# A hybrid transformer on one core: 64 unused bytes on the left of SBUF and 96 on the right shift every tile

## The chip, the cores and the metric

One core of a Trainium2 chip runs the whole program in one launch. The metric is the device time of that core in microseconds (us), as a median of several executions; lower is better. A profile of one execution gives start and duration of every instruction on TensorE (PE for its matmuls, PEld for its weight loads), VectorE (DVE), ScalarE (ACT) and GpSimd (POOL), and the transfers of the DMA queues.

## The reference

Two layers of a transformer on 512 tokens with 1024 features, all in float32. Each layer is a half-weighted feed-forward network (FFN), a mixer, and a second half-weighted FFN, each behind an RMS norm. The first mixer joins gated linear attention (4 heads) with forgetting attention (8 heads); the second is sparse attention in a latent space (16 heads, a top-k of the keys).

```python
def swiglu(h, w_in, w_out):
    a, b = jnp.split(h @ w_in, 2, axis=-1)
    return (jax.nn.silu(a) * b) @ w_out          # w_in 1024 x 5632, w_out 2816 x 1024
...
    for layer in range(DEPTH):
        g = norm_g[layer]
        x = x + 0.5 * swiglu(rmsnorm(x, g[0]), ffn_w_in[layer, 0], ffn_w_out[layer, 0])
        h = rmsnorm(x, g[1])
        x = x + (even_mixer if layer % 2 == 0 else odd_mixer)(h, ...)
        x = x + 0.5 * swiglu(rmsnorm(x, g[2]), ffn_w_in[layer, 1], ffn_w_out[layer, 1])
    return rmsnorm(x, final_norm_g)
```

(The loop is shortened: the two mixers take weights of their own.)

## The kernel before, in words

The stages run one after the other: FFN 0, even mixer, FFN 1, FFN 2, odd mixer, FFN 3, final norm. Tokens lie along the free dimension of a tile, features on the 128 partitions.

**Three products for one.** An operand is split into a high part of type float32r (a rounded float32 that TensorE takes at its full rate) and a low part, and a product is the sum of high x high, high x low and low x high. `mm3` (line 204) issues these three for the FFN's down product and for the mixers' projections; the FFN's up product does the same at line 366. Weights are fetched by SP's queue into raw tiles (`wraw`, `a`), split by ScalarE (`whi`) and VectorE (`wlo`, lines 84 and 88, 162 and 163), and become the stationary operand. Each matmul is preceded by a weight load of its own.

**The FFN's up product** is a seven-product scheme for 2x2 blocks: eleven rounds (pairs of hidden tiles), each with seven products `p1` to `p7` of 24 matmuls over 256 columns, all of them from line 366. Their moving operands are the tiles `th` and `tl` (high and low part of the input blocks). **The down product** multiplies the tiles `hh` and `hl` in matmuls over 512 columns (lines 207 to 209).

**The mixers** first project: the input `xgh`, `xgl` is the moving operand over 512 columns, or, for values, the stationary one with the weights moving over 256 columns. Attention and output products follow; their tiles are called `x`, `p` and `pts`.

**Where tiles lie.** A partition of SBUF is filled from both ends. Pools on the left are stacked upwards: the pool `one` (residual `X`, gains `gn` of 224 bytes, `ones`, `ident`, masks, `cols` of 32 bytes), then the small tiles of the norms, then `wraw`, `wsp` (which holds `whi` and `wlo`), and in their stage `hp` (`hh`, `hl`) or the mixers' pools. The one pool on the right, `xp`, hangs from the upper end: `th` and `tl`, or `xgh` and `xgl`, the raw weight tiles `a` and the work tiles `ws`, `te`, `to`. Small tiles are no multiples of 128 bytes, so that what follows them starts between two multiples. In the program before, `X` starts at byte 16,512, `ss` at 35,200, and the highest tile of the right side ends at byte 229,344 of its partition.

Where an operand starts, modulo 128 bytes, for all 12,006 matmuls of the program:

| matmuls (type, columns that move) | count | stationary, moving before |
|---|---|---|
| FFN up, float32r, 256 | 7,224 | 64, 96 |
| FFN down, mixers' `x` tiles, float32r, 512 | 2,640 | 64, 64 |
| projections of `xgh`/`xgl` (720) and FFN 0's first products (96), float32r, 512 | 816 | 64, 96 |
| mixers' values, float32r, 256 (stationary `xgh`/`xgl`) | 384 | 96, 64 |
| other float32r (scores, narrow projections) | 240 | 64, 64 or 96, 96, narrow ones mixed |
| float32 (transposes, attention values, norms) | 702 | mixed |

Of the kernel before, what the change touches and what calls it, by code (L numbers as in the profile page):

```python
# [8 lines left out]
F32 = mybir.dt.float32  # L9
# [163 lines left out]
class Builder:  # L173
# [1090 lines left out]
    def build(self):  # L1264
        from contextlib import ExitStack
        with ExitStack() as ctx:
            nc, tc = self.nc, self.tc
            pool = lambda name, bufs, **kw: ctx.enter_context(tc.tile_pool(name=name, bufs=bufs, **kw))
# [6 lines left out]
            self.pp = pool("pp", 1, space=PSUM)  # L1275
            self.dram = pool("dram", 1, space=bass.MemoryType.DRAM)
            one = lambda name, shape, dt=F32: self.one.tile(shape, dt, name=name)
            self.lnexp()
            self.X = one("X", [128, KT, S])
            self.gn = one("gn", [128, 7, KT])  # L1280
# [7 lines left out]
            for t, n in ((self.chunkmask, "chunkmask"), (self.ident, "ident"), (self.causal, "causal"), (self.cols, "cols")):  # L1288
                nc.gpsimd.dma_start(t, self.i[n])

            self.xp = None

            def open_in(kind):
# [173 lines left out]
```

## Time and profile before

| | before |
|---|---|
| median of three runs | 1914.0 us (1907.32 to 1915.86) |
| profiled execution, its own time | 1906.54 us |
| its span in the profile | 1904.7 us |
| instructions in the profile | 30516 |
| mean granted TensorE clock | 0.991 |

The span is what the profiler sees from the first to the last instruction; the execution's own time has some 2 us around it. A granted clock of 1 is the upper of TensorE's two levels (2.4 GHz), 0.5 the lower (1.2 GHz). The duration that the profile gives for one matmul contains its way through the array and overlaps with the next one's: what a matmul costs in a dense stretch is the distance from its start to the start of the next.

### The profile page before, as it was taken

Reading aid. Unit: us, or ns where it says so; the run is one execution under the profiler, and the core shown is the slowest. Engines: PE = TensorE matmul, PEld = TensorE weight load, DVE = VectorE, ACT = ScalarE, POOL = GpSimd, SP = SyncE. Lnnn points to the kernel's source line nnn. Section 1 sums busy time; section 2 is a strip of 40 time slices with the busy share of each in tenths; the row PEclk is TensorE's granted clock in tenths of the full one; section 3 lists DMA queues with packets and bytes.
Section 4 is the critical chain, followed back from the end, with each engine's and each line's share of the span. In section 5 each row is a group of like instructions: output and inputs, shape, how many; then the busy total and the mean of one; then the engine's idle time right before and its main releaser. Section 6 shows DMA issues by size and latency. Waiting matters only on the chain.

```text
span 1904.7 us, 30516 instructions
## 1 busy us (share of the span) xinstructions
PE 1858.3 (98%) x12376; PEld 1665.6 (87%) x12376; DVE 1451.5 (76%) x1917; ACT 909.9 (48%) x1286; POOL 218.0 (11%) x211
## 2 busy tenths in 40 slices
PE   8999999999999999999999999999999999999997
PEld 7989899887877999989899998987777789899996
DVE  8979687457557979868897885964898599696774
ACT  6535345334465634525564452543538566353353
POOL 0000000100262000000200000011258320000001
PEclk9999999999999999999999999999999999999998
DMA  5333422223441233322423333234156222423322
GB/s 186 96 107 105 126 86 78 94 80 96 126 122 67 89 110 104 113 97 78 144 89 92 109 100 122 67 107 136 60 162 170 79 94 93 125 89 114 108 67 78
DMA packets 60653, 198.16 MB, mean 104 GB/s; under 512 B 7896, under 2 KB 8072, under 8 KB 57440
## 3 DMA queue, kind: packets, MB, share of 16 engines
q1 hardware_dynamic: 57856, 191.65, 32.2%
q10 hardware_dynamic: 2304, 4.20, 0.8%
q8 instruction: 97, 1.59, 0.3%
q0 software_dynamic: 352, 0.36, 0.1%
q14 instruction: 44, 0.36, 0.1%
HBM read 178.03 MB, written 2.15 MB: 95 GB/s over the span
## 4 chain that ended last, share of the span: by engine, by line
PE 84%; DVE 12%; ACT 2%; issue 1%; DMA 1%; SPq 0%; DVEq 0%; POOL 0%; ACTq 0%; POOLq 0%
PE ps L366 25%; PE pt L366 12%; PE s L209 6%; PE s L208 6%; PE s L207 6%; PE s L366 6%; PE ps L207 3%; PE ps L208 3%; PE ps L209 3%; PE s L730 2%; DVE tl L241 2%; DVE wlo L88 1%; PE o L764 1%; DVE acc L1217 1%; PE pt L749 1%; PE pt L207 1%
## 5 line engine op out<-in xcount | busy, mean ns | idle before, releaser
L366 PE MATMUL ps<-th,wlo 128*128 128x256 f32 x1376 | 384.8, 280 | 2.4 <-DVE wlo L163 2.3
L366 PE MATMUL ps<-th,whi 128*128 128x256 f32 x1376 | 385.2, 280 | 1.3 <-DVE ta L414 1.3
L366 PE MATMUL ps<-tl,whi 128*128 128x256 f32 x1376 | 384.5, 279 | 0.9 <-DVE tl L241 0.9
L84 ACT ACTIVATE whi<-wraw 128x1024 fp32r<-128x1024 f32 (+3 forms) x156 | 157.3, 1010 | 351.0 <-PE s L208 135.5
L366 PEld LDWEIGHTS ps<-th,wlo 128*128 128x128 f32 x1376 | 259.4, 188 | 3.2 <-DVE wlo L163 3.2
L366 PEld LDWEIGHTS ps<-th,whi 128*128 128x128 f32 x1376 | 259.2, 188 | 2.3 <-DVE ta L414 1.5
L366 PEld LDWEIGHTS ps<-tl,whi 128*128 128x128 f32 x1376 | 259.3, 188 | 1.7 <-DVE tl L241 1.1
L209 PE MATMUL s<-hh,wlo 128*128 128x512 f32 x528 | 205.9, 390 | 0.0
L208 PE MATMUL s<-hl,whi 128*128 128x512 f32 x528 | 205.6, 389 | 0.0
L207 PE MATMUL s<-hh,whi 128*128 128x512 f32 x528 | 205.6, 389 | 0.0
L162 ACT ACTIVATE whi<-a 128x1024 fp32r<-128x1024 f32 x131 | 139.0, 1061 | 137.8 <-issue 39.2
L88 DVE TENSOR_TENSOR wlo<-wraw,whi 128x1024 fp32r<-128x1024 f32 (+3 forms) x144 | 169.2, 1176 | 40.3 <-ACT whi L84 39.8
L279 POOL TENSOR_TENSOR ss<-ss,sq 128x512 f32<-128x512 f32 x41 | 65.4, 1596 | 1113.6 <-ACT sq L275 1113.4
L366 PE MATMUL pt<-th,whi 128*128 128x256 f32 x688 | 192.0, 279 | 0.0
L366 PE MATMUL pt<-tl,whi 128*128 128x256 f32 x688 | 191.9, 279 | 0.0
L366 PE MATMUL pt<-th,wlo 128*128 128x256 f32 x688 | 191.9, 279 | 0.0
L163 DVE TENSOR_TENSOR wlo<-a,whi 128x1024 fp32r<-128x1024 f32 x131 | 159.7, 1219 | 6.8 <-ACT whi L162 6.7
L162 ACT ACTIVATE whi<-wraw 128x1024 fp32r<-128x1024 f32 (+1 forms) x89 | 93.6, 1052 | 131.7 <-PE ps L366 51.5
L492 DVE SCALAR_TENSOR_TENSOR dn<-s,R 128x512 f32<-128x512 f32 x72 | 49.7, 690 | 122.3 <-PE s L209 122.3
L162 ACT ACTIVATE whi<-ws 128x1024 fp32r<-128x1024 f32 x86 | 90.7, 1055 | 84.0 <-PE ps L366 51.2
L366 PEld LDWEIGHTS pt<-tl,whi 128*128 128x128 f32 x688 | 129.3, 188 | 0.0
L366 PEld LDWEIGHTS pt<-th,wlo 128*128 128x128 f32 x688 | 129.3, 188 | 0.0
(323 smaller groups left out, 4338.4 us busy)
## 6 DMA issues: line engine op xcount, KB each, us to landing
a<-in_ffn_in_dram SPq DMA_DIRECT2D x88, 512.0 KB, 3.7
wraw<-in_ffn_in_dram SPq DMA_DIRECT2D x87, 512.0 KB, 4.7
wraw<-in_ffn_out_dram SPq DMA_DIRECT2D x64, 512.0 KB, 3.6
wraw<-in_ffn_out_dram SPq DMA_DIRECT2D x32, 384.0 KB, 3.1
x<-x SPq DMA_DIRECT2D x62, 128.0 KB, 2.3
wraw<-in_even_fox_dram SPq DMA_DIRECT2D x4, 1024.0 KB, 4.8
wraw<-in_even_out_dram SPq DMA_DIRECT2D x4, 1024.0 KB, 5.6
wraw<-in_odd_q_dram SPq DMA_DIRECT2D x8, 512.0 KB, 3.2
```

Of the source, the lines that this page charges most:

```text
L84: nc.scalar.activation(hi, x, AF.Copy)
L88: nc.vector.tensor_sub(lo, x, hi.bitcast(F32))
L162: b.nc.scalar.activation(o[0][:, s], x[:, s], AF.Copy)
L163: b.nc.vector.tensor_sub(o[1][:, s], x[:, s], o[0][:, s].bitcast(F32))
L207: mm(ps, w[0], x[0], start=first, stop=False)
L208: mm(ps, w[0], x[1], start=False, stop=False)
L209: mm(ps, w[1], x[0], start=False, stop=last)
L241: v.tensor_sub(l, src, h.bitcast(F32))
L279: nc.gpsimd.tensor_tensor(self.ss, self.ss, sq, op=OP.add)
L366: mm(o, w[:, c], x, start=fresh and f == j == i == 0, stop=j == 3 and i == 2, skip_group_check=True)
L492: nc.vector.scalar_tensor_tensor(t, bank, 0.5, R, op0=OP.mult, op1=OP.mult)
L730: nc.tensor.matmul(s[:, :n], q[hh][:, b * 128:b * 128 + 128], k[hh][:, :n], start=k is kh, stop=k is kl)
```

## The change

Two tiles are added that no instruction writes or reads. `edge_l` is the first tile of the pool `one`, 16 float32 = 64 bytes of each partition, and pushes all tiles of the left side up by 64 bytes. `edge` lies in a pool of its own on the right side, 24 float32 = 96 bytes, opened ahead of `xp`, and pushes all tiles of the right side down by 96 bytes.

```diff
             one = lambda name, shape, dt=F32: self.one.tile(shape, dt, name=name)
+            one("edge_l", [128, 16])
             self.lnexp()
             self.X = one("X", [128, KT, S])
...
+
+            pool("edge", 1, side="right").tile([128, 24], F32, name="edge")
             self.xp = None
```

Each engine has the same instructions in the same order with the same waits as before; only addresses in SBUF differ (PSUM and DRAM are as before). `X` now starts at byte 16,576, the highest tile on the right ends at 229,248, a multiple of 128. Of the table above, the first four rows and nearly all of the fifth now have stationary and moving operand at 0, 0: all 11,064 matmuls of the first four rows and 210 of the fifth's 240; the other 30 (of the projections 48 and 72 columns wide) start their stationary operand at another multiple of 32 bytes, their moving operand at 0 too. Operands of float32 moved as well, and not all of them to a multiple: `ident` goes from 96 to 32, `ones` from 96 to 32, `ss` from 0 to 64. `X`, which ScalarE, VectorE and GpSimd use and TensorE doesn't, goes from 0 to 64.

## Rows read from the trace of the kernel before

**Rows 1.** The page: engines' busy time, and the chain that ended last, by engine.
```profile
PE 1858.3 (98%) x12376; PEld 1665.6 (87%) x12376; DVE 1451.5 (76%) x1917; ACT 909.9 (48%) x1286; POOL 218.0 (11%) x211
...
PE 84%; DVE 12%; ACT 2%; issue 1%; DMA 1%; SPq 0%; DVEq 0%; POOL 0%; ACTq 0%; POOLq 0%
```

**Rows 2.** Stretches of time: length, busy us by engine, granted clock, DMA share, GB/s.
```profile
350.00:610.00 260.00, 253.98 (x1513) 207.07 (x1512) 156.28 (x273) 118.26 (x223) 57.02 (x80) 0.99 0.31 98
...
841.00:900.00 59.00, 59.00 (x479) 57.79 (x478) 50.59 (x51) 30.08 (x33) 0.00 (x0) 1.00 0.20 64
...
1300.00:1560.00 260.00, 245.26 (x1406) 194.12 (x1405) 204.01 (x455) 140.30 (x309) 112.47 (x93) 0.97 0.42 118
```

**Rows 3.** Groups by line and shape: count, busy us, mean ns, idle before.
```profile
L366 PE MATMUL ps<-th,whi 128*128 128x256 f32 x1376 | 385.2, 280 | 1.3 <-DVE ta L414 1.3
...
L209 PE MATMUL s<-hh,wlo 128*128 128x512 f32 x528 | 205.9, 390 | 0.0
...
L207 PE MATMUL ps<-xgh,whi 128*128 128x512 f32 x208 | 84.2, 405 | 0.0
...
L207 PE MATMUL ps<-whi,xgh 128*128 128x256 f32 x128 | 37.6, 294 | 0.0
```

**Rows 4.** Timeline of PE, FFN up, first and last of 34 matmuls.
```profile
1800.09 0.28 PE L366 MATMUL pt<-th,wlo 128*128 128x256 f32 x1
...
1803.94 0.28 PE L366 MATMUL ps<-th,wlo 128*128 128x256 f32 x1
```

**Rows 5.** Timeline of PE, even mixer's output product, first and last of 28 matmuls.
```profile
599.76 0.39 PE L207 MATMUL ps<-x,whi 128*128 128x512 f32 x1
...
605.88 0.39 PE L207 MATMUL ps<-x,whi 128*128 128x512 f32 x1
```

**Rows 6.** Timeline of PE, even mixer's projections, first and last of 58 matmuls.
```profile
439.65 0.40 PE L207 MATMUL ps<-xgh,whi 128*128 128x512 f32 x1
...
452.95 0.39 PE L207 MATMUL ps<-xgh,whi 128*128 128x512 f32 x1
```

**Rows 7.** Timeline of PE, even mixer's values, first and last of 38 matmuls.
```profile
381.28 0.28 PE L209 MATMUL ps<-whi,xgl 128*128 128x256 f32 x1
...
385.66 0.28 PE L207 MATMUL ps<-whi,xgh 128*128 128x256 f32 x1
```

**Rows 8.** Stretches: 512 columns at the lower clock; FFN up with transfers under way.
```profile
1359.90:1360.80 0.90, 0.90 (x3) 0.66 (x2) 0.58 (x1) 0.06 (x1) 0.00 (x0) 0.50 0.00 0
...
1800.00:1804.00 4.00, 4.00 (x37) 4.00 (x36) 3.30 (x4) 1.64 (x3) 0.00 (x0) 1.00 0.79 266
```

**Rows 9.** Timeline of PE at that lower clock, first and last of 3 matmuls.
```profile
1359.98 0.63 PE L207 MATMUL ps<-x,whi 128*128 128x512 f32 x1
...
1360.84 0.47 PE L209 MATMUL ps<-x,wlo 128*128 128x512 f32 x1
```

**Rows 10.** Timeline of PE, begin of FFN 0's down product: matmuls 1, 4 and 10.
```profile
93.51 0.40 PE L207 MATMUL s<-hh,whi 128*128 128x512 f32 x1
...
94.21 0.39 PE L207 MATMUL s<-hh,whi 128*128 128x512 f32 x1
...
95.57 0.39 PE L207 MATMUL s<-hh,whi 128*128 128x512 f32 x1
```

**Rows 11.** Timeline of PE, odd mixer: scores of 256 columns between projections.
```profile
1328.70 0.40 PE L1227 MATMUL s<-x 128*128 128x256 f32 x2
1328.94 0.40 PE L207 MATMUL ps<-xgh,whi 128*128 128x512 f32 x1
```

**Rows 12.** Timeline of PE, a norm's sums: one moving column each, eight weight loads.
```profile
624.06 0.95 PE L314 MATMUL o<-ones,ss 128*128 128x1 f32 x8
624.96 0.39 PE L366 MATMUL ps<-th,whi 128*128 128x256 f32 x1
```

## The prediction

> **What bounds the kernel now.** I read the page first. TensorE is busy for 98% of the span, VectorE for 76%, and 84% of the chain that ended last is matmuls [rows 1]. By stretches, an FFN's up product keeps TensorE busy without a gap at a granted clock of 1.00 (59.00 of 59 us), while VectorE has 50.59 us, 86%; the stretch with the even mixer leaves 260 - 254 = 6 us free, the one with the odd mixer 260 - 245 = 15 us [rows 2]. So the time is a count of matmuls times the distance between their starts, and the next engine is 14% away where most of them lie. Four groups of shapes hold 11,064 of the 12,006 matmuls [rows 3]; their operand offsets are in the table above.
>
> The timeline gives the distance of each group.
> - FFN up, 256 columns, offsets 64 (stationary) and 96 (moving): (1803.94 - 1800.09) / 33 = 116.7 ns [rows 4].
> - Output product, 512 columns, offsets 64 and 64: (605.88 - 599.76) / 27 = 226.7 ns [rows 5].
> - Projections, 512 columns, offsets 64 and 96: (452.95 - 439.65) / 57 = 233.3 ns [rows 6].
> - Values, 256 columns, offsets 96 and 64: (385.66 - 381.28) / 37 = 118.4 ns [rows 7].
>
> The second and third line are the finding. Same shape, same stationary offset, same clock; the moving operand at 96 instead of 64 costs 6.7 ns, 3%. At 2.4 GHz the three regular streams are 280, 544 and 560 cycles: per 32 columns (128 bytes) 35, 34 and 35. 560 is twice 280, so at offset 96 a column costs the same at either width, and the moving operand sets the pace there, not the weight load, which is 128 columns in both. At the lower clock the extra vanishes: 512 columns at a granted 0.50 take (1360.84 - 1359.98) / 2 = 430 ns, 516 cycles of 1.2 GHz within the rounding of the rows [rows 8, 9]. So in the dense streams something that feeds TensorE, not the array, is the limit, and the offset is part of it. Transfers are not: the 116.7 ns stand in a stretch with 266 GB/s under way [rows 4, 8].
>
> **The change part by part.** No instruction is added, removed or moved, no wait and no DMA; two idle tiles take memory alone and cost nothing. What changes is the offset of operands, group by group.
>
> FFN up, 7,224 matmuls: (64, 96) becomes (0, 0). No row shows an operand of float32r at 0. The nearest is a pair with equal offsets, 64 and 64, at 34 cycles per 32 columns; I take that rate, since a shift of both operands by the same 64 bytes leaves their distance as it is. 256 columns then take 226.7 / 2 = 113.3 ns, 3.3 ns less: 7,224 x 3.33 = 24.1 us. From below the gain is 0, if at 256 columns the next weight load sets the pace. From above the weight load by itself bounds it: with one moving column, eight loads take (624.96 - 624.06) / 8 = 112 ns each [rows 12], so at most 4.7 ns and 34 us.
>
> Projections, 816 matmuls: 233.3 becomes 226.7 ns by the rows that differ in nothing else. 96 of them open FFN 0, where TensorE waits for its operands; I count the other 720: 4.8 us.
>
> Values, 384 matmuls: 118.4 becomes 113.3 ns, as above: 1.9 us.
>
> Down and output products, 2,640 matmuls: (64, 64) becomes (0, 0). By the rate that I took: nothing. The bound below is a loss: such a stream needs some matmuls to reach its pace, (94.21 - 93.51) / 3 = 233.3 ns for the first three of a down product and (95.57 - 94.21) / 6 = 226.7 ns for the next six [rows 10]; if it never settled, 2,640 x 6.7 = 17.6 us would be lost. The bound above is an array that is never held up, 512 / 2.4 = 213.3 ns: 13.4 x 2,640 = 35 us won.
>
> [...]
>
> The rest: float32 operands, 702 matmuls, of which the transposes' `ident` goes from 96 to 32, lie in attention, where TensorE has its idle time; ScalarE's and VectorE's operands move too, but VectorE's 14% and ScalarE's half of the time cover a change of some per cent there. I count neither. If VectorE's cover were gone, that is its rate became 14% worse, a round of the FFN would wait for it.
>
> Sum: 24.1 + 4.8 + 1.9 = 30.8 us of TensorE. An FFN up round has 168 matmuls, 19.6 us; at 19.0 us VectorE's 86% become 88%, so no new bound arises, but waits at stage ends and in the two mixers don't shrink; I take 30. Against the profiled execution's own 1906.5 us (span 1904.7) that is 1876.5. That execution lies 7.5 us below the median of the runs, 1914.0, and half a per cent (some 9.6 us) is about what a measurement of this kernel can tell from no change, its three runs being 8.5 us apart. Against the median: **1884 us**.
>
> **The rivals.**
> - *Zero is better than 64.* If the surplus of 2 cycles per 32 columns comes from a boundary at each multiple of 128 bytes that a moving operand at 64 or 96 straddles, it falls or goes at 0. For: 34 and 35 of 32 show a surplus to be had, and it is larger for the worse offset. Against: no row has offset 0, and (64, 64) may already be the aligned case. With half of the surplus gone, 220 ns for 512 columns and the load's 112 ns for 256: 6.7 x 2,640 + 13.3 x 720 + 4.7 x 7,224 + 6.4 x 384 = 17.7 + 9.6 + 34.0 + 2.5 = 64 us, **1850 us**; with all gone 35 + 14.4 + 34 + 2.5 = 86 us, 1828. [...]
> - *The weight load paces the 256-column stream.* Then FFN up stays at 116.7 ns and only projections and values gain, 6.7 us: **1907 us**, within half a per cent. For: a pair of 256-column matmuls at 64 and 64 in the odd mixer takes (1328.94 - 1328.70) / 2 = 120 ns, no less than at 96 [rows 11], and the values, whose moving operand is at 64, take 118.4 [rows 7]. Against: the pair stands alone between projections, and streams need three matmuls to settle [rows 10]; the values' stationary operand is at 96; and 280 is exactly half of 560.
> - *Offsets have nothing to do with it*, and the 6.7 ns come from something else: **1914 us**. For: every tile at 64 lies on the left side, every one at 96 on the right, so side and offset are not told apart here. Against: tiles of different pools, stages and writers agree, `x` with `hh` at 226.7 ns [rows 5, 10], `xgh` with `th` at one cost per column [rows 4, 6].
> - *The 512-column streams no longer settle* at (0, 0), and the up product gains nothing: + 17.6 us, **1932 us**, slower. It decides from some 1,440 of the 2,640 matmuls on (9.6 us at 6.7 ns). For it: the pace depends on how two streams fall together, since it changes within nine matmuls [rows 10]. Against: the distance of the two offsets, the one thing that could set it, stays 0.
>
> **How the numbers follow.** The forecast has a chance of 0.42, zero better than 64 0.20, the load as the pace 0.22, no effect 0.05, never settled 0.11. Faster by over 0.5% are the first two, 0.62; within it the next two, 0.27; slower 0.11. The forecast's own range is 1875 to 1893 (31 us less a few, and the scatter of the runs). To leave out no more than 2 in 10, the range runs from 1840, which holds half or more of the second case, to 1912, which holds the third: below it some 0.07 are left, above it the last case and part of the fourth.
>
> **What would show it.** Right: in the profile after, 113.3 ns between starts of the up product's matmuls, 226.7 in projections, output and down products alike, VectorE's share in the up product near 88%, and the same instruction counts. 112 or less at 256 columns, and under 226 at 512, show the second case; 116.7 at 256 with 226.7 at 512 in the projections the third. Wrong would also be a distance that falls as said while the time doesn't, with new idle time ahead of line 366 released by VectorE.

## The result: 0.8% slower

| | before | after |
|---|---|---|
| median | 1912.96 us (4 runs, 1907.32 to 1915.86) | 1929.03 us (4 runs, 1925.98 to 1929.58) |
| profiled execution, its own time | 1906.54 us | 1929.58 us |
| its span | 1904.7 us | 1927.8 us |
| instructions | 30516 | 30516 |

The ratio is 1.0084, with an interval of 1.0058 to 1.011: slower by more than the half per cent that can be told from no change. The forecast was 1884 us, faster by 1.6%.

The page of the changed kernel, busy time by engine and the chain that ended last:

```profile
PE 1881.4 (98%) x12376; PEld 1689.4 (88%) x12376; DVE 1454.0 (75%) x1917; ACT 909.9 (47%) x1286; POOL 217.0 (11%) x211
...
PE 84%; DVE 11%; ACT 2%; issue 1%; DMA 1%; POOL 0%; SPq 0%; DVEq 0%; ACTq 0%; POOLq 0%
```

Against [rows 1] TensorE is busy 23.1 us longer with the same number of instructions, and the span is 23.1 us longer; VectorE, ScalarE and GpSimd stay within 3 us. The busy time of as many matmuls grew, and not the gaps between them: the same matmuls stand farther apart. Which of them, the timeline of TensorE shows (start, duration), the first and last of 34 matmuls of the up product, 28 of the output product, 58 of the projections and 38 of the values, as in [rows 4 to 7]:

```profile
1821.22 0.28 PE L366 MATMUL pt<-th,wlo 128*128 128x256 f32 x1
...
1825.18 0.28 PE L366 MATMUL ps<-th,wlo 128*128 128x256 f32 x1
...
606.69 0.39 PE L208 MATMUL ps<-x,whi 128*128 128x512 f32 x1
...
612.81 0.39 PE L208 MATMUL ps<-x,whi 128*128 128x512 f32 x1
...
440.57 0.39 PE L208 MATMUL ps<-xgl,whi 128*128 128x512 f32 x1
...
453.81 0.40 PE L208 MATMUL ps<-xgl,whi 128*128 128x512 f32 x1
...
383.75 0.28 PE L208 MATMUL ps<-wlo,xgh 128*128 128x256 f32 x1
...
388.14 0.28 PE L209 MATMUL ps<-whi,xgl 128*128 128x256 f32 x1
```

- FFN up: (1825.18 - 1821.22) / 33 = 120.0 ns, where [rows 4] gave 116.7.
- Output product: (612.81 - 606.69) / 27 = 226.7 ns, as in [rows 5].
- Projections: (453.81 - 440.57) / 57 = 232.3 ns, against 233.3 in [rows 6]; an unbroken run of 168 in the odd mixer has a mean of 233.3 ns in both kernels.
- Values: (388.14 - 383.75) / 37 = 118.6 ns, against 118.4 in [rows 7].

That the 120.0 ns hold throughout a stretch is seen by counting. In 60 us of FFN 1's up product, windows of the kernel before and of the changed one (columns as in [rows 2]):

```profile
740.00:800.00 60.00, 60.00 (x517) 60.00 (x516) 53.66 (x54) 33.82 (x38) 0.00 (x0) 1.00 0.33 102
```
```profile
740.00:800.00 60.00, 60.00 (x502) 60.00 (x501) 54.57 (x54) 32.68 (x36) 0.00 (x0) 1.00 0.30 97
```

A window of 60 us touches (60 + 0.28) / pace matmuls, so 517 is 116.6 ns and 502 is 120.1, both without a gap and at a granted clock of 1.00. This window is the measure used for the kernels below.

Where the 23 us arose, by stages, each from the start of its first product to the start of the next stage's, FFN 3 to the start of its last down product (from the timelines; one execution of each kernel, the experiments of the next section included):

```
            FFN 0   even    FFN 1+2   odd     FFN 3  | FFNs     mixers
before      347.1   261.3   679.7     256.8   338.5  | 1365.3   518.1
after       350.1   265.8   690.7     256.4   343.6  | 1384.4   522.2
l64         348.3   265.5   684.2     256.4   341.4  | 1373.9   521.9
r32         350.5   260.1   690.0     257.1   344.2  | 1384.7   517.2
r96         345.1   267.3   678.1     257.3   337.8  | 1361.0   524.6
same32      347.4   264.1   679.6     256.0   338.4  | 1365.4   520.1
r96m        346.0   264.5   678.4     259.8   337.7  | 1362.1   524.3
r96k        340.3   265.8   671.7     258.3   335.5  | 1347.5   524.1
d32k        345.8   267.5   678.9     259.5   338.7  | 1363.4   527.0
```

The FFNs took 19.1 us more, the mixers 4.1. An FFN has 1,176 up matmuls behind a down product, at 120.0 instead of 116.7 ns, and some 500 more behind its norm, at 118.8 instead of 116.8 (means that include a long first step): 3.9 + 1.0 = 4.9 us, and FFN 3 took 5.1 more. The windows behind FFN 1's norm, before and after:

```profile
645.00:690.00 45.00, 45.00 (x388) 45.00 (x387) 40.44 (x40) 24.20 (x27) 0.00 (x0) 1.00 0.32 100
```
```profile
645.00:690.00 45.00, 45.00 (x382) 45.00 (x381) 42.45 (x43) 27.18 (x30) 0.00 (x0) 1.00 0.25 82
```

The 4.5 us of the even mixer are within scatter: d32k, whose mixers lie at the addresses of before, took 267.5 us for it where before took 261.3. The profiled executions are 23 us apart and the medians 16, because the profiled one of before lies 6.4 us below its median and that of after 0.6 above.

### The profile page after: what moved, and what is told of

It reads as the page before. It is cut to its first block, busy times and chain, and to the rows that moved or that the text cites. A ratio compares the mean times of both kernels' runs of the same rounds, so it can differ in the third digit from the quotient of the medians.

```text
span 1927.8 us, 30516 instructions
## 1 busy us (share of the span) xinstructions
PE 1881.4 (98%) x12376; PEld 1689.4 (88%) x12376; DVE 1454.0 (75%) x1917; ACT 909.9 (47%) x1286; POOL 217.0 (11%) x211
## 4 chain that ended last, share of the span: by engine, by line
PE 84%; DVE 11%; ACT 2%; issue 1%; DMA 1%; POOL 0%; SPq 0%; DVEq 0%; ACTq 0%; POOLq 0%
PE ps L366 25%; PE pt L366 12%; PE s L207 6%; PE s L209 6%; PE s L208 6%; PE s L366 6%; PE ps L207 3%; PE ps L208 3%; PE ps L209 3%; PE s L730 2%; DVE tl L241 1%; PE o L764 1%; DVE wlo L88 1%; DVE acc L1217 1%; PE pt L749 1%; PE pt L207 1%
## 5 line engine op out<-in xcount | busy, mean ns | idle before, releaser
L366 PE MATMUL ps<-th,wlo 128*128 128x256 f32 x1376 | 391.1, 284 | 2.3 <-DVE wlo L163 2.3
L366 PE MATMUL ps<-tl,whi 128*128 128x256 f32 x1376 | 389.9, 283 | 0.0
L366 PEld LDWEIGHTS pt<-th,whi 128*128 128x128 f32 x688 | 130.4, 190 | 0.0
```

Of the source, the lines that this page charges most:

```text
L366: mm(o, w[:, c], x, start=fresh and f == j == i == 0, stop=j == 3 and i == 2, skip_group_check=True)
```

## The experiments

Three theories of what sets the pace of a dense stream. **Own offset**: where each operand starts modulo 128 bytes, as the prediction had it. **Side**: which end of SBUF it lies at. **Distance**: the start of the moving operand minus that of the stationary one, modulo some power of two. Of the third the change did something that its table of offsets modulo 128 doesn't show. It pushed the left side up by 64 and the right side down by 96, so the distance of the up product went from 32 to 32 - 160 = -128, which modulo 256 is 128; both operands start at multiples of 128 bytes now, but one at an even, the other at an odd multiple. The projections go from 32 to 128 with it; the values, whose stationary operand is the one on the right, go from 224 to 128. Output and down products have both operands on the left, and stay at 0.

**A map of the pace (map1).** Streams of 36 matmuls from line 53, with no work for another engine between them; 256 or 512 columns, distance 0 to 992 bytes in steps of 32, some with both operands shifted by the same `a`, some with the moving operand 82 KB away (the code is shortened, its constants written out).

```python
for name, n, d, a in streams():
    w0 = PADF + a // 4
    m0 = PADF + a // 4 + 2048 + d // 4
    for i in range(36):
        c = w0 + (i % 8) * 128
        nc.tensor.matmul(ps[:, :n], big[:, c:c + 128], big[:, m0:m0 + n], start=i == 0, stop=i == 35)
```

> A kernel of dense matmul streams alone (36 matmuls each, one weight load per matmul, no other engine at work); it computes nothing of the reference and writes its input out. Stationary chunks start at multiples of 512 bytes, the moving operand d bytes further modulo 1024, d from 0 to 992 in steps of 32, with 256 and with 512 columns; further streams shift both operands by 32, 64 and 96 bytes at d = 0, or put the moving operand 82 KB away. Theory 'distance': the pace is set by d alone, with some period; d = 0, 32 and 384 at 512 columns repeat the kernels' 226.7, 233.3 and 233.3 ns, d = 32 and 384 at 256 columns their 116.7 and 120.0 ns, and shifting both operands changes nothing. Theory 'own offset': the streams with both operands shifted by 32, 64, 96 differ from each other by 3 to 7 ns at 512 columns, and d matters only through the moving operand's own offset modulo 128, so the pace repeats every 128 bytes. Theory 'side': with both operands in one tile all streams run at 226.7 ns, and only the far ones at 233.3.

Measured: rows of the timeline, one for a whole stream (start, time from its first start to its last end). The name gives columns, distance and `a`:

```profile
30.51 4.43 PE L53 MATMUL n256d128a0x<-big 128*128 128x256 f32 x36
39.00 4.28 PE L53 MATMUL n256d192a0x<-big 128*128 128x256 f32 x36
421.07 4.47 PE L53 MATMUL n256d000a64x<-big 128*128 128x256 f32 x36
433.89 4.48 PE L53 MATMUL n256far000x<-big 128*128 128x256 f32 x36
149.27 8.35 PE L53 MATMUL n512d000a0x<-big 128*128 128x512 f32 x36
157.46 8.57 PE L53 MATMUL n512d032a0x<-big 128*128 128x512 f32 x36
```

Less the last one's duration (0.28 us, and 0.39 and 0.40 at 512 columns) and over 35 steps: 118.6 and 114.3 ns at 128 and 192, 119.7 with both operands at 64 modulo 128, 120.0 with the moving operand 82 KB away; (8.35 - 0.39) / 35 = 227.4 ns for 512 columns at distance 0, 233.4 at 32. Worked out from the last 16 steps of each stream, in ns:

```
distance modulo 256       0      32     64     96     128    160    192    224
256 columns             120.0  117.6  117.8  120.1  118.7  117.3  113.3  118.3
512 columns             226.7  233.3  228.9  233.6  233.3  234.7  233.3  233.3
```

The distances up to 992 repeat this row four times, all but the very first stream (distance 0, 256 columns), which took 7.23 us, a mean of 198.6 ns a step, and is left out; the first matmuls of the kernel before are slow too, (8.57 - 7.29) / 3 = 427 ns for 512 columns in a window with a granted clock of 1.00. Shifting both operands by 32, 64 or 96 at distance 0 changes nothing (120.0 and 226.7 ns), and being 82 KB apart changes less than half a nanosecond. So own offset and side fall, and distance modulo 256 bytes stands. Two things didn't come out as the theory of distance had it: 32 and 128 gave 117.6 and 118.7 ns at 256 columns where the kernels have 116.7 and 120.0, and with both operands shifted by 64 the stream at 32 ran at 116.7. So a distance can have more than one rate, which the experiments below take up. The map also contradicts what the prediction took for granted, that the two widths go together. Distance 0 is the best for 512 columns and among the two slowest for 256.

**One pad alone (l64, r96, r32).** The whole kernel with the left pad alone (distance of the up product 224), with the right pad alone (192), and with 32 bytes on the right instead of 96, which puts both operands at 64 modulo 128 and the distance at 0: in all stages, the pair of equal offsets that the prediction took for its rate. The three lines, one for each kernel in this order, against before:

```diff
+            one("edge_l", [128, 16])
...
+            pool("edge", 1, side="right").tile([128, 24], F32, name="edge")
...
+            pool("edge", 1, side="right").tile([128, 8], F32, name="edge") 
```

> The left pad alone: stationary at 0, moving at 96 in the up product (distance 480 modulo 512), 512-column down product at 0 and 0. Theory 'own offset, stationary at 0 is slow': up product at 120 ns, time as after the change, 1929 us. Theory 'own offset, moving at 0 is slow': 116.7 ns, 1913 us. Theory 'distance': the up product takes a value of its own that the map shows at d = 480; down product unchanged at 226.7.

> The right pad alone: stationary at 64, moving at 0 in the up product (distance 448 modulo 512), down product at 64 and 64. Theory 'own offset, stationary at 0 is slow': 116.7 ns, 1913 us. Theory 'own offset, moving at 0 is slow': 120 ns, 1929 us. Theory 'distance': the value of the map at d = 448.

> A right pad of 32 bytes alone: both operands of all large groups at 64 modulo 128, and their distance 0 modulo 512. Theory 'distance': up product and projections take the pace of the output products, 226.7 ns at 512 columns and so 113.3 at 256, 30 us won, 1883 us; if the weight load paces the 256-column stream, up to 120 ns there and 24 us lost, less 5 won in the projections, 1932 us. Theory 'own offset': since 64 and 64 is as bad or good as the mean of the two single shifts, between 1913 and 1929 us. Theory 'side': no change, 1913 us.

Measured: l64 1919.57 us, ratio 1.0056 (1.0038 to 1.0073); r96 1908.45 us, 1.0003 (0.9989 to 1.0017); r32 1928.62 us, 1.0108 (1.0079 to 1.0136). The window of the up product in l64, then r32:

```profile
740.00:800.00 60.00, 60.00 (x510) 60.00 (x509) 55.33 (x55) 32.87 (x37) 0.00 (x0) 1.00 0.31 97
```
```profile
740.00:800.00 60.00, 60.00 (x502) 60.00 (x501) 54.50 (x54) 32.19 (x37) 0.00 (x0) 1.00 0.32 97
```

60.28 / 510 = 118.2 ns at distance 224, 60.28 / 502 = 120.1 at distance 0: the map's numbers (118.3 and 120.0). The times of l64 and r96 alone don't tell the theories apart: l64 lies between own offset's two forecasts, 1913 and 1929 us, and r96 near the lower one. r32 decides about the prediction's step. Its up product has equal offsets, and is as slow as the changed kernel's, so 256 columns don't take half of what 512 take. Its projections did gain: the timeline of r32, first and last of 58,

```profile
440.27 0.40 PE L209 MATMUL ps<-xgh,wlo 128*128 128x512 f32 x1
...
453.21 0.39 PE L209 MATMUL ps<-xgh,wlo 128*128 128x512 f32 x1
```

are (453.21 - 440.27) / 57 = 227.0 ns apart in place of 233.3 [rows 6].

r96 has two rates at one distance. Windows of FFN 1's up product behind the norm and behind the down product, and of FFN 2's behind the down product:

```profile
645.00:690.00 45.00, 45.00 (x400) 45.00 (x399) 43.20 (x44) 26.14 (x30) 0.00 (x0) 1.00 0.29 90
740.00:800.00 60.00, 60.00 (x512) 60.00 (x511) 54.60 (x55) 33.26 (x37) 0.00 (x0) 1.00 0.32 100
...
1075.00:1135.00 60.00, 60.00 (x512) 60.00 (x511) 55.56 (x55) 32.94 (x37) 0.00 (x0) 1.00 0.32 97
```

45.28 / 400 = 113.2 ns behind the norm, where the first step is 207 ns long, but 60.28 / 512 = 117.7 behind the down product, where the stream follows without a gap. Same operands, same distance: distance alone has no room for that. Something in how a stream begins must choose.

**How a stream begins (map2).** Each stream of 72 matmuls of 256 columns now follows 15 matmuls of 512 columns at distance 0, as the up product follows the down product. The stationary operands start at 64 modulo 128, as in before; in map1 they start at 0. Some have one or more narrow matmuls at line 52 in between (the code is shortened, its constants written out).

```python
for i in range(15):
    mm(head, big[:, c:c + 128], big[:, m0:m0 + 512], start=i == 0, stop=i == 14)
for n in kick:                       # (), (2,), (2,)*4, (64,), (128,), (128, 128), (192,), (384,)
    mm(ps[:, :n], big[:, w0:w0 + 128], big[:, m:m + n], start=True, stop=True)
for i in range(72):
    c = w0 + (i // 3 % 8) * 128
    mm(ps[:, :256], big[:, c:c + 128], big[:, m:m + 256], start=i == 0, stop=i == 71)
```

> Dense streams alone again, nothing of the reference: 15 matmuls of 512 columns at distance 0 (modulo 256, as the down product ends), then at once 72 matmuls of 256 columns at a distance of 0 to 224; then distance 192 and 32 once more with a few extra short matmuls (2 to 384 columns) between the two streams. Theory 'distance modulo 256 alone': each stream takes the map's value (120.0, 117.6, 117.8, 120.1, 118.7, 117.3, 113.3, 118.3 ns for 0 to 224), with or without the extra ones. Theory 'distance and the way in' (a stream can settle in more than one rhythm): at 192 the stream behind the 512 columns stays at 117.8 ns, as in the kernel with the right pad alone, where up products behind a norm ran at 113.5 and those behind a down product at 117.8; some of the extra matmuls bring it to 113.3.

Measured, rows as in map1, at distance 192 without and with one matmul of 64 columns ahead:

```profile
87.50 8.64 PE L55 MATMUL d192x<-big 128*128 128x256 f32 x72
...
147.85 0.19 PE L52 MATMUL d192one64x<-big 128*128 128x64 f32 x1
147.88 8.43 PE L55 MATMUL d192one64x<-big 128*128 128x256 f32 x72
```

(8.64 - 0.28) / 71 = 117.7 ns without; with it (8.43 - 0.28) / 71 = 114.8, in which the first step counts 204 ns, and the last 16 steps are 113.3. So the second rate is a second steady rhythm of the same stream, and the way in chooses it. At 192, two matmuls of 128 columns, one of 192 and one of 384 do it too (means of 114.1, 113.9 and 113.5 ns); one, two or four of 2 columns and one of 128 don't (118.6 to 119.0). At distance 32 the way in counts too, and there an extra matmul did harm: one of 2 or of 128 columns made 117.6 or 117.7 ns of 116.6. The eight distances behind 512 columns, and what the up product does at each in whole kernels, last steps in ns:

```
distance modulo 256        0      32     64     96     128    160    192    224
map2, 256 columns        120.0  116.6  117.8  120.1  120.0  118.5  117.8  118.4
kernels, up product      120.0  116.7    -      -    120.0    -    117.8  118.3
                          r32   before               after          r96    l64
```

All five distances agree, though map2's program has no work for VectorE, ScalarE or a transfer between its streams, and also where the stationary operand starts at 0 instead of map2's 64 (after, l64). Behind the norms the kernels show map1's other rhythms: 118.8 ns at 128 (after), 113.5 at 192 (r96), means that include the long first step.

**The same distance by other pads (same32).** Left 64, and on the right 192 bytes in the FFNs alone: both operands of the up product at other places than before, its distance 32 again.

```diff
+            one("edge_l", [128, 16])
...
+                if kind == "ffn":
+                    self.xe = tc.alloc_tile_pool(name="xe", bufs=1, side="right", reuse_waits="tile")
+                    self.xe.tile([128, 48], F32, name="edge_f")
```

> Left pad of 64 bytes, and a right pad of 192 bytes in the FFN stages alone: stationary at 0, moving at 32 modulo 128, so both have other offsets than before, but their distance in the up product is 32 modulo 256, as before. Theory 'distance': the up product takes 116.7 ns and the time is that of before within half a per cent, 1909 us. Theory 'own offset': not before's; with the stationary operand at 0, as in the left pad alone, 118 to 120 ns and 1919 to 1929 us.

Measured: 1907.17 us, 0.9981 (0.9966 to 0.9996). The window of the up product:

```profile
740.00:800.00 60.00, 60.00 (x517) 60.00 (x516) 55.51 (x56) 32.93 (x37) 0.00 (x0) 1.00 0.31 97
```

517 as before. One operand is at a multiple of 128 bytes now, and the pace is that of before: in the kernel too it is the distance that counts. One stretch differs, the one behind FFN 1's norm, which ran at 117.8 ns here and at 116.7 in before: distance 32 has a second rate in a kernel too, near the 117.6 of map1.

**Best distance for each stage (r96m).** Right pad 96 in the FFNs, 32 in the mixers, so that the projections stand at distance 0.

```diff
+            pool("edge", 1, side="right").tile([128, 8], F32, name="edge")
...
+                if kind == "ffn":
+                    self.xe = tc.alloc_tile_pool(name="xe", bufs=1, side="right", reuse_waits="tile")
+                    self.xe.tile([128, 16], F32, name="edge_f")
```

> Right pad of 96 bytes in the FFN stages, 32 in the mixers: distance 192 in the up product, 0 in the down product and in the projections. Theory 'distance': up product as in the right pad alone (113.5 and 117.8 ns), projections at 226.7 in place of 233.3 ns (4.8 us won), values at 120 in place of 118 (0.8 us lost): 4 us under the right pad alone, 1904 us. Theory 'own offset': projections unchanged at 233.3, 1908 us.

Measured: 1910.45 us, 0.9998 (0.998 to 1.0016). The gain that the projections should bring isn't there; the values went to 120.0 ns as forecast. In the odd mixer the place is seen: the window of 168 projections in r96m and the same ones in r96, then two of the waits that stand in r96m's:

```profile
1382.90:1422.90 40.00, 39.00 (x170) 31.31 (x169) 39.24 (x93) 12.20 (x16) 18.56 (x12) 1.00 0.58 165
```
```profile
1384.90:1424.30 39.40, 39.40 (x172) 31.58 (x170) 38.65 (x93) 12.27 (x17) 19.83 (x13) 1.00 0.62 175
```
```profile
1399.22 0.39 PE L209 MATMUL ps<-xgh,wlo 128*128 128x512 f32 x1
1400.44 0.47 PE L207 MATMUL ps<-xgh,whi 128*128 128x512 f32 x1 [0.83 <-DVE x L1138]
...
1405.29 0.39 PE L207 MATMUL ps<-xgh,whi 128*128 128x512 f32 x1
1405.51 0.39 PE L208 MATMUL ps<-xgl,whi 128*128 128x512 f32 x1
1405.74 0.39 PE L209 MATMUL ps<-xgh,wlo 128*128 128x512 f32 x1
1406.19 0.47 PE L207 MATMUL ps<-xgh,whi 128*128 128x512 f32 x1
```

The matmuls stand 0.23 us apart as forecast, and then one comes 1.22 us, another 0.45 us after the last. The profile names VectorE (line 1138) as what ended the longest of these waits, and VectorE is busy for 39.24 of the 40 us. In r96 it is as busy, but TensorE has no gap; with its matmuls closer together TensorE gets ahead and waits. Three such steps (1.22, 0.45 and 0.49 us in place of 0.23) and the slower ones right behind them cost 1.7 us, more than the 168 x 6.7 ns = 1.1 us won. r32, whose projections have the same distance, waits at the same three places (1.22, 0.41 and 0.49 us). In the even mixer (264.5 us against 267.3 in r96) any gain is within the scatter of the table by stages.

**Narrower weight loads (map3).** If the surplus is two reads that collide, that of the moving operand and that of the next weights, a load of fewer columns should leave less of it. The streams of map1 with loads of 128, 64, 32 and 8 columns, which leaves that many rows of output.

```diff
-                nc.tensor.matmul(ps[:, :n], big[:, c:c + 128], big[:, m0:m0 + n], start=i == 0, stop=i == MM - 1)
+                nc.tensor.matmul(ps[:m, :n], big[:, c:c + m], big[:, m0:m0 + n], start=i == 0, stop=i == MM - 1)
```

> Dense streams alone, nothing of the reference: distances 0, 32, 96, 128, 192 with 256 and 512 moving columns, and weight loads of 128, 64, 32 and 8 columns. Theory 'two reads collide' (the extra cycles arise where the load of the next stationary operand and the moving operand are read at once): with narrower loads the extra shrinks and the distance ceases to matter; at 8 columns every distance runs within 2 ns of the others, near 213 ns at 512 columns and 107 at 256. Rival 'the moving operand alone': the extra stays what it is at 128 columns (227 to 234 ns) down to 8.

Measured, rows as in map1:

```profile
29.56 4.24 PE L42 MATMUL n256m128d192x<-big 128*128 128x256 f32 x36
...
75.41 4.37 PE L42 MATMUL n256m8d000x<-big 128*8 128x256 f32 x36
...
92.00 4.24 PE L42 MATMUL n256m8d192x<-big 128*8 128x256 f32 x36
...
221.18 8.33 PE L42 MATMUL n512m8d000x<-big 128*8 128x512 f32 x36
229.35 8.50 PE L42 MATMUL n512m8d032x<-big 128*8 128x512 f32 x36
```

(4.24 - 0.28) / 35 = 113.1 ns at 192 with loads of 128 and of 8 columns alike; the best stream of either width has the same pace at 128 columns as at 8. The last 16 steps over the distances 0, 32, 96, 128 and 192 in ns:

```
load, columns        128              64               32               8
256 columns     113.3 to 120.0  113.3 to 119.2   113.3 to 117.5   113.3 to 116.7
512 columns     226.7 to 233.4  229.7 to 232.6   230.1 to 233.6   226.6 to 231.7
```

(The stream at distance 0 with loads of 128 stood first and took 7.19 us, a mean of 197.4 ns a step; its 120.0 is map1's.) Each row's best and worst aren't at the same distances, though: at 256 columns distance 0 is among the slowest with loads of 128 columns and among the fastest, at 113.3, with 64 and 32; 192 is the fastest down to 64, slower with 32 (116.7) and back at 113.3 with 8, where 96 and 128 stand at 113.3 too. The forecast of two reads that collide fails: a load of a sixteenth doesn't bring 256 columns below 113.3 ns, nor 512 below 226.6. That floor goes with the columns that move, 113.3 for 256 and twice that for 512, and not with the width of the load. The rival, that the extra stays what it is, fails as well: at 256 columns the spread over the distance shrinks from 6.7 to 3.4 ns, and which distance is fast changes with the load. So the load has a part in what lies on top of the floor; how, isn't shown.

**The better rhythm in the kernel (r96k, d32k).** r96 with one more matmul of 64 columns ahead of the first up product behind each of the eight down products; its result is overwritten by the product that follows. And d32k: before, distance 32, with the same eight; the diff's last line is r96k's alone.

```diff
                     d = st[p] = {"a": self.bank("ps")}
+                    if p in (4, 8):
+                        mm(d["a"][:, :64], W.parts[p, q][0][:, :128], TH[0][:, B11][:, :64], start=True, stop=True, skip_group_check=True)
                     product(p, q, d["a"], B11, True)
...
+            pool("edge", 1, side="right").tile([128, 24], F32, name="edge")
```

> The right pad of 96 bytes alone (distance 192 in the up product), and one extra matmul of 64 columns ahead of the up product behind each of the first two down products of an FFN, eight in all; its sum is overwritten. Theory 'distance and the way in': the up products behind down products, 4 x (672 + 504) = 4,704 matmuls, go from 117.8 to 113.3 ns, 21 us won against the right pad alone: 1887 us, 1.1 to 1.2% under the kernel before. Rival 'distance alone': the 117.8 ns there have another reason (load of other engines), nothing changes, 1908 us.

> The kernel before, no pad, with the same eight extra matmuls. If the extra matmul by itself brought something, it would show here; by the second map at distance 32 the stream has two rhythms, 116.6 and 117.6 ns, so between nothing and 4,704 x 1.0 = 5 us lost: 1910 to 1915 us.

Measured: r96k 1893.47 us (6 runs), ratio 0.9913 (0.9894 to 0.9932); d32k 1910.01 us, 1.0000 (0.9983 to 1.0017). The begin of a stretch in r96k, with the added matmul at line 442:

```profile
721.45 0.39 PE L209 MATMUL s<-hh,wlo 128*128 128x512 f32 x1
721.67 0.19 PE L442 MATMUL ps<-th,whi 128*128 128x64 f32 x1
721.70 0.36 PE L366 MATMUL ps<-th,whi 128*128 128x256 f32 x1
721.91 0.28 PE L366 MATMUL ps<-tl,whi 128*128 128x256 f32 x1
722.02 0.28 PE L366 MATMUL ps<-th,wlo 128*128 128x256 f32 x1
```

and a window behind a down product in r96k, then in d32k:

```profile
1075.00:1135.00 60.00, 60.00 (x532) 60.00 (x531) 54.87 (x55) 33.21 (x38) 0.00 (x0) 1.00 0.35 108
```
```profile
1075.00:1135.00 60.00, 60.00 (x516) 60.00 (x516) 56.00 (x55) 33.20 (x38) 0.00 (x0) 1.00 0.31 97
```

60.28 / 532 = 113.3 ns where r96 had 512 in the same window, 117.7; all eight such stretches of r96k run at this rate. At distance 32 the same edit does nothing (516, 116.8 ns). So it isn't the added matmul by itself, but the rhythm that it opens at this distance. r96k is faster than both kernels of this document, 1.0 - 0.9913 = 0.9% below the one before; the FFNs gave 1365.3 - 1347.5 = 17.8 us. It fell some 6 us short of what was forecast for it, partly because the way in isn't under control elsewhere: the first stretches of FFN 2 and 3 behind their norms, 113.5 ns in r96, came out at 117.9 in this execution, 504 x 4.4 ns = 2.2 us each.

## Why the prediction was wrong

- **What bounds the kernel: right.** The span grew by as much as TensorE's busy time, 23.1 us, and VectorE's and ScalarE's moved operands, which the prediction counted at nothing, changed nothing that shows: 1454.0 and 909.9 us busy, within 3 us of [rows 1]. The counts of instructions and the granted clock in the FFNs (1.00 in the windows above) are as before.
- **"FFN up ... I take that rate, since a shift of both operands by the same 64 bytes leaves their distance as it is. 256 columns then take 226.7 / 2 = 113.3 ns": this step failed, twice.** The first half is true by itself (map1: a shift of both changes nothing) but was applied to offsets modulo 128, when the pace goes by the distance modulo 256; there (0, 0) isn't (64, 64), but 128 away from it. The second half fails even at distance 0: r32 and map1 give 226.7 ns at 512 columns and 120.0 at 256. The halving rested on "560 is twice 280", which is so at distance 32 (233.3 and 116.7 ns) and at neither 0 nor 192 (233.3 and 113.3). The term of 24.1 us became a loss of some 19.
- **"From below the gain is 0": a loss was shut out without a reason.** The pair at equal offsets in [rows 11] took 120 ns, the very pace of 256 columns at distance 0 in map1. One pair, read to 10 ns, is no more than a hint, and the prediction set it aside as one that stood alone; but no row of it shut a loss out.
- **Projections, 4.8 us: failed by the same step.** Distance 128 leaves them at 232.3 to 233.3 ns. At distance 0 (r32, r96m) they do run at 227, but in the odd mixer VectorE's 98% turned the gain into a wait.
- **Values, 1.9 us: failed by the same step**, 118.6 ns against 118.4; they went from distance 224 to 128.
- **Down and output products, nothing: right**, 226.7 ns; both operands moved together.
- **"the weight load paces the 256-column stream": wrong in that form.** 113.3 ns is reached with full loads (r96, r96k, map1). The load has a part in the spread (map3), not in the floor.
- **"Offsets have nothing to do with it": wrong**, and so is *zero is better than 64* (map1: 120.0 ns at either).
- **The rival that ends slower had the right sign, 1932 us, by the wrong group.** The 512-column streams settled as before; the streams of 256 columns lost. That its number lies 3 us from the measured median is luck.

That the changed kernel's 120.0 ns come from the distance is shown: by r32 and map2, which reach it at the distances 0 and 128 by other addresses, and by same32, which returns to 116.7 with others still. What inside the chip makes the distance count, and why a way in chooses between two rhythms, stays open.

## What to carry to other kernels

Aligning both operands of a dense matmul stream to a round number is no aim in itself; what changes its pace here is the distance between moving and stationary start modulo 256 bytes, by up to 6%, with a best value that differs by width (192 bytes for 256 columns, 0 for 512, of the steps of 32 bytes tried, with loads of 128 columns). A rate read at one width is not halved for another: a small kernel of bare streams at the candidate distances, each behind what precedes it in the real kernel, gave the right number for the up product behind a down product in all five layouts. When only one stage's streams gain, look first at whether the next engine there has room, as VectorE hadn't in the odd mixer.

## What the runs showed of the hardware

- **A floor of 113.3 ns for 256 columns of float32r and 226.6 for 512.** Neither a stream of the maps nor a dense stretch read in the kernels (granted 1.00 in the windows) went below it by more than the rounding of the rows, with loads of 8 columns or 128 (map3). At a granted 0.50, 512 columns took 430 ns [rows 8, 9]; by the ratio of the clocks that would be 215 ns at 1.00 and 107.5 for 256 columns, an estimate from three matmuls read to 10 ns. The prediction's cycles, 2.4 per ns at 1.00, fit it (512 / 215 = 2.38); the 213.3 ns that it gives an array that is never held up stays an estimate, which no stream reached. Operands of float32 took longer: 512 columns at lines 1008 and 1125 of the kernel before stand 1.02 - 0.59 = 0.43 us apart, also at 1.00.
- **The start distance modulo 256 bytes** moves a dense stream, with loads of 128 columns, between 113.3 and 120.1 ns at 256 columns and between 226.7 and 234.7 at 512 (map1).
- **One stream has several steady rhythms**, 113.3 and 117.8 ns at distance 192, which it keeps for hundreds of matmuls (532 in a window of r96k, 512 in the same window of r96); a single matmul of 64 columns ahead of it switches (117.7 to 114.8 ns in the mean of map2's 72), one of 128 doesn't (118.6).
